# A hybrid RWKV-7 / mLSTM layer: scans in written order on every engine, and finishing work cut into parts

## The chip, the cores and the metric

The kernel runs on one core of a Trainium2 chip: TensorE (PE) for matmuls, VectorE (DVE), ScalarE (ACT), GpSimd (POOL), and SyncE (SP), which here only issues DMAs. The metric is the device time of one execution in microseconds; lower is better. Every number below is in us unless it says ns.

## The reference, cut to what matters

One layer of a bidirectional trunk over 128 context and 1024 latent tokens. A modulated RMSNorm feeds one input projection; its columns go to an RWKV-7 mixer, an mLSTM mixer and two sigmoid gates. Both mixers scan forward and backward; the latent scans start from states.

```
S = S*w_t - (S kk_t)(kk_t a_t)^T + v_t k_t^T;  y_t = S r_t          # RWKV-7, per head, both directions
y = group_norm(y_fwd + y_bwd) * lnx_g + lnx_b;  (y + bonus) * g
h = num / max(|den|, exp(-m));  C' = decay*C + sum_j w_j v_j k_j^T   # mLSTM, chunk of positions
h = group_norm(h_fwd + h_bwd) * gn_g * sigmoid(o)
merged = sigmoid(z_g)[r] * (y_r @ W_r) + sigmoid(z_g)[m] * (y_m @ W_m)
```

After that come an output projection, a residual and a gated convolution FFN.

## The kernel before, in words

Projections are computed with every weight split into a high and a low part (`whi` on ACT, `wlo` on DVE) and three products, 24 matmuls for one column group of 128. The regions of the program are: preparation and the first projections (to about 620 on the trace's time line), the RWKV scan (634 to 957), the mLSTM scan (971 to 1122), the rest of the gate products and the branches, then the FFN. The change touches the two scans alone.

**RWKV scan.** There are 18 steps n; each takes one chunk of 64 tokens per direction. `loads(n, d)` brings KA (two 128 KB DMAs), BKs and four TT pieces on SP, and XN on POOL's queue. KA comes from a ring of four buffers, two per step, so the loads for step n+1 need the buffers whose last reader is pY of step n-1. `scores(n+1, d)` makes psc and pbk of the coming step; ACT and DVE copy and mask them into A, KA, AB and BT. `merge` makes pmh and pmt (TT). `back(n)` is the recurrence: pP, pU (into suv), pN (into sn and the next suv), pY (into ysum). `between(n)` places the scores, the merge and the *gate products* (`fill(2)`: 2 times 12 matmuls pg of the 24 of a column group f, whose sigmoid goes to zraw and sgz) among the phases of `back`.

**Work carried by the scan.** `gates()` is a generator of six stages, called after steps 3, 4, 5, 6, 8 and 10, that prepares the mLSTM gates: small DMAs on SP (gi, gf, red, rr, mpd, mc, Mrd, dcd, decb), scans on DVE and Exp/Ln on ACT. `rpost(b)` finishes a block of 128 tokens of RWKV output (mean, variance, power on POOL, pgg and pgt on PE, yt): a first part after the step in POST, a second part in the next step's `between`.

**mLSTM scan.** There are 18 iterations i. `mfront` (two iterations ahead) adds the mask on POOL, takes Exp on ACT (MI), makes pmP and pmk, scales kw on ACT and multiplies MI by S on DVE. `mback` makes pmN and pmC, den, hs (h or hsum) and CN. `mfinish(c)` (from i = 10 on, and once at i = 1) makes mu on DVE, four squares on ACT (sqm), va, a power on POOL, h3, pmf and som.

**What sets the order.** PE's instructions keep the written order during both scans. On DVE, ACT, POOL and SP a scheduler chose the order at build time, except that the gate stages were kept in order (`pinned(gate)`). An instruction waits at the head of its engine's queue, and everything behind it on that engine waits too.

Of the kernel before, what the change touches and what calls it, by code (L numbers as in the profile page):

```python
# [16 lines left out]
NB = 9  # L17
# [40 lines left out]
def _body(tc, ctx, A, O, dbg, stop):  # L58
# [80 lines left out]
    Mrd = dram("Mrd", [2, 2, 36, 128])  # L139
# [225 lines left out]
    def split_w(srcs, nk, ncol, pool_=None, tag="w", bufs=2):  # L365
# [6 lines left out]
        nsplit[0] += 1  # L372
        if pool_ is None:
# [7 lines left out]
        return hi, lo  # L381

# [358 lines left out]
    def zg_groups(fs):  # L741

        w2s = {}

        def load(f):
            w2s[f] = split_w([kp(w_in[:, 3984 + 128 * f:4112 + 128 * f])], 8, 128)

        for i, f in enumerate(fs):
            if f not in w2s:
                load(f)  # L750
            sg = stage()
            for g in range(3):
# [19 lines left out]
    banks(pg=2, ps=3, pf=3)  # L772
# [10 lines left out]
    rp = pool("rpost", 1, mpc)  # L783
    cpc = ExitStack()
# [119 lines left out]
    def back(n, qs, suv, suv_next, parts):  # L904
# [57 lines left out]
    def rpost(b):  # L962
# [14 lines left out]
        gp.tensor_tensor(va, va, mhalf, op=ALU.pow)  # L977
        v.tensor_tensor(y, y, va.unsqueeze(2).to_broadcast([128, 8, 64]), op=ALU.mult)
        yield
        bon = rp.tile([128, 4, 128], F32, name="bon", tag="bon")  # L980
        pdma(bon, bond[:, :, bs].rearrange("p c t -> c p t"))
        for p in range(4):
            s.activation(bon[:, p, :], bon[:, p, :], AF.Identity, bias=P("rwkv_lnx_b", p))
# [14 lines left out]
        v.tensor_tensor(yt, pgg, yt, op=ALU.mult)  # L998
        pdma(yrd[:, :, bs].rearrange("p c t -> c p t"), yt)
# [5 lines left out]
    def gates():  # L1005
# [94 lines left out]

    def between(n):

        if n + 1 == len(ORDER):
            for i in range(3):
# [11 lines left out]
        if due:  # L1116
            due.pop(0)()
        fill(2)
# [13 lines left out]
    gate, due = gates(), []  # L1132
    pe.on = True
    for n in range(len(ORDER)):
# [3 lines left out]
        if n > 0 and n + 1 < len(ORDER):  # L1138
            fr[n + 1] = [loads(n + 1, d) for d in range(2)]
        sn = back(n, fr.pop(n), suv, None if n == 1 else nxt, between(n))  # L1140
        suv = nxt
        if n == 1:
            due.append(lambda sn=sn: finish_ctx(sn))
        if n in POST:
            r = rpost(POST[n])
            next(r)
            due.append(lambda r=r: next(r))
        if n in (3, 4, 5, 6, 8, 10):
            pinned(gate)
# [42 lines left out]
    def mload(d, c):  # L1192
        q = Chunk()
        q.d, q.c, q.vx = d, c, None
        q.qk = mp.tile([128, 8, 128], F32, name="qk", tag="qk", bufs=3)
        dma(q.qk, qkd[c])
        q.MI = mp.tile([128, 2, 4, 128], F32, name="MI", tag="MI", bufs=4)
        for x in range(2):
            src = Mrd[x, d].rearrange("(h c) t -> h c t", c=NB)[:, c, :]
            dma(q.MI[:, x], src.unsqueeze(0).to_broadcast([128, 4, 128]))  # L1200
        return q

    def values(q, dma_):
        q.vx = mp.tile([128, 4, 130], F32, name="vx", tag="vx", bufs=2)
        dma_(q.vx[:, :, 0:128], vmd[q.c])
        gp.memset(q.vx[:, :, 128:129], 1.0)

    def mfront(q):
# [3 lines left out]
        if q.vx is None:  # L1212
            values(q, dma)

        gp.tensor_tensor(dm, dm, mbig[:, d:d + 1, :].to_broadcast([128, 4, 128]), op=ALU.add)
        for h in range(4):
            s.activation(dm[:, h, :], dm[:, h, :], AF.Exp, scale=-1.0, bias=cols(gT[0], d, c)[:, h:h + 1])
# [50 lines left out]
    def mfinish(c):  # L1268
        h3 = hs_of(c)
# [3 lines left out]
        sq = mf.tile([128, 4, 128], F32, name="sqm", tag="sqm")  # L1273
        va = mf.tile([128, 4], F32, name="va", tag="va")
        for h in range(4):
            s.activation(sq[:, h, :], h3[:, h, :], AF.Square, bias=mu[:, h:h + 1], accum_out=va[:, h:h + 1])
        v.tensor_scalar(va, va, 1.0 / 128, 1e-5, op0=ALU.mult, op1=ALU.add)
        gp.tensor_tensor(va, va, mhalf[:, 0:4], op=ALU.pow)
        for h in range(4):
            v.tensor_scalar(h3[:, h, :], h3[:, h, :], mu[:, h:h + 1], va[:, h:h + 1], op0=ALU.add, op1=ALU.mult)  # L1280
        so = mf.tile([128, 4, 128], F32, name="som", tag="sqm")
        dma(so, sod[c])
# [4 lines left out]
        for h in range(4):  # L1287
            v.scalar_tensor_tensor(so[:, h, :], pt[:, h, :], P("mlstm_gn_g", h), so[:, h, :],
                                   op0=ALU.mult, op1=ALU.mult)
        dma(ymd[:, :, 128 * c:128 * c + 128].rearrange("h p t -> p h t"), so)  # L1290
# [39 lines left out]
    qs = [mload(*dc) for dc in SEQ[0:3]]  # L1330
    for q in qs[0:2]:
        values(q, pdma)
    sts = [state_loads(d) for d in range(2)]
    rps = [rpost(b) for b in (1, 8)]
    next(rps[0])
    for q in qs[0:2]:
        mfront(q)
    next(rps[1])
    fill(2)
    fins, half = [], []  # L1340
    for i, (d, c) in enumerate(SEQ):
# [287 lines left out]
```

## Time and profile before

| what | value |
|---|---|
| median of 3 runs (lowest to highest) | 2233.98 (2229.5 to 2241.99) |
| profiled execution, its own time | 2238.79 |
| its span (first to last instruction) | 2237.1 |
| PE busy, share of the span | 2086.1, 93% |
| DVE / ACT / POOL busy | 1374.4 / 818.7 / 569.2 |
| granted TensorE clock, mean | 0.972 |

The span is 1.7 below the execution's own time. Busy PE includes matmuls slowed by a lower clock, so PE's busy time is not its shortest time.

### The profile page before, as it was taken

How to read it: one execution, taken by the hardware profiler on the slowest of the kernel's cores; microseconds unless marked ns; L12 is line 12 of the kernel's file. 1: busy time of each engine (PE TensorE's matmuls, PEld its weight loads, DVE VectorE, ACT ScalarE, POOL GpSimd, SP SyncE). 2: the span in 40 equal slices, each digit the busy share in tenths (PEclk: the TensorE clock that was granted, in tenths of full speed). 3: DMA queues.
4: the chain of work that ended last, by engine and by line, in shares of the span. 5: the costliest groups of instructions: out<-in, count | busy, mean ns of one | idle time of the engine just before them, and what ended most of it. 6: DMA issues, size and time to landing. Idle time of an engine off the chain costs nothing. (4 is left out here: it accounts for less than half of the span.)

```text
span 2237.1 us, 39684 instructions
## 1 busy us (share of the span) xinstructions
PE 2086.1 (93%) x16307; PEld 1933.2 (86%) x16307; DVE 1374.4 (61%) x2131; ACT 818.7 (37%) x1595; POOL 569.2 (25%) x726
## 2 busy tenths in 40 slices
PE   5999998998888988979889999999999999999998
PEld 3998898888887877868878978999999999999996
DVE  3766688879745656563733365655565556565658
ACT  3664746364234433345431143522222222212223
POOL 2000098888722224255412212000000000000004
PEclk8999999999999999989999999999999999999999
DMA  9135354545555555367677552111111111111114
GB/s 267 50 83 134 100 138 108 144 122 143 151 146 133 137 133 137 110 201 217 194 250 199 162 188 76 57 57 48 47 48 57 48 48 48 57 39 44 41 57 169
DMA packets 387189, 256.67 MB, mean 115 GB/s; under 512 B 90529, under 2 KB 362053, under 8 KB 387008
## 3 DMA queue, kind: packets, MB, share of 16 engines
q1 hardware_dynamic: 239824, 140.96, 22.4%
q10 hardware_dynamic: 137056, 88.83, 13.5%
q0 software_dynamic: 10128, 24.35, 4.0%
q8 instruction: 128, 2.10, 0.4%
q14 instruction: 53, 0.43, 0.1%
HBM read 188.82 MB, written 65.25 MB: 114 GB/s over the span
## 5 line engine op out<-in xcount | busy, mean ns | idle before, releaser
L393 PE MATMUL pg<-act,whi 128*128 128x384 f32 (+1 forms) x3808 | 724.6, 337 | 0.5 <-DVE act L356 0.4
L393 PEld LDWEIGHTS pg<-act,whi 128*128 128x128 f32 (+1 forms) x3808 | 665.7, 188 | 12.7 <-DVE act L356 0.7
L393 PE MATMUL pg<-act,wlo 128*128 128x384 f32 (+1 forms) x1904 | 373.1, 336 | 7.6 <-DVE wlo L380 7.6
L393 PEld LDWEIGHTS pg<-act,wlo 128*128 128x128 f32 (+1 forms) x1904 | 332.9, 187 | 11.1 <-DVE wlo L380 8.0
L380 DVE TENSOR_TENSOR wlo<-wraw,whi 128x1024 fp32r<-128x1024 f32 x130 | 162.8, 1254 | 226.7 <-ACT whi L379 221.2
L47 DVE SCALAR_TENSOR_TENSOR ua<-uraw,par,ua 128x945 f32<-128x945 f32 (+2 forms) x176 | 214.6, 1219 | 39.0 <-ACT ua L1514 35.8
L1593 POOL TENSOR_TENSOR x<-facc,grow 128x512 f32<-128x512 f32 x16 | 23.5, 1490 | 809.1 <-DMA x<-x1d 799.0
L393 PE MATMUL pfd<-whi,f 128*128 128x512 f32 x792 | 226.1, 394 | 0.2 <-ACT f L1528 0.2
L379 ACT ACTIVATE whi<-wraw 128x1024 fp32r<-128x1024 f32 x130 | 136.7, 1053 | 158.2 <-PE pg L393 85.3
L393 PEld LDWEIGHTS pfd<-whi,f 128*128 128x128 f32 x792 | 147.0, 188 | 28.8 <-issue 1.6
L1591 DVE TENSOR_TENSOR facc<-pfd,facc 128x512 f32<-128x512 f32 x162 | 110.3, 686 | 50.6 <-PE pfd L393 50.6
L540 POOL TENSOR_TENSOR Lb<-Lb,tmp 96x31 f32<-96x31 f32 (+15 forms) x155 | 130.3, 841 | 12.2
L538 POOL TENSOR_TENSOR tmp<-La,Lb 96x31 f32<-96x31 f32 (+15 forms) x155 | 122.9, 793 | 27.4 <-DMA La<-Ad 15.6
L393 PE MATMUL pfd<-wlo,f 128*128 128x512 f32 x396 | 122.7, 391 | 0.0
L1518 ACT ACTIVATE ua<-ua 128x1152 f32<-128x1152 f32 x22 | 25.7, 1169 | 221.5 <-DVE ua L47 221.5
L69 PE MATMUL pg<-act,whi 128*128 128x384 f32 x496 | 103.3, 360 | 0.0
L1528 ACT ACTIVATE f<-ua 128x384 fp32r<-128x384 f32 x66 | 32.1, 518 | 192.9 <-DVE ua L1527 192.9
L69 PEld LDWEIGHTS pg<-act,whi 128*128 128x128 f32 x496 | 91.2, 202 | 1.1
L47 DVE SCALAR_TENSOR_TENSOR qacc<-zraw,par,qacc 128x945 f32<-128x945 f32 (+2 forms) x64 | 86.6, 1353 | 8.7 <-ACT qacc L596 8.2
L1462 PE MATMUL pwo<-whi,act 128*128 128x512 f32 x288 | 90.1, 392 | 1.1 <-ACT whi L379 1.1
L872 DVE TENSOR_TENSOR KA<-psc,msk 64x512 f32<-64x512 f32 x72 | 49.3, 684 | 66.4 <-ACT A L871 66.1
L393 PEld LDWEIGHTS pfd<-wlo,f 128*128 128x128 f32 x396 | 74.3, 188 | 16.5
(398 smaller groups left out, 3280.1 us busy)
## 6 DMA issues: line engine op xcount, KB each, us to landing
wraw<-in_w_in ACTq DMA_DIRECT2D x44, 512.0 KB
wraw<-in_ffn_up ACTq DMA_DIRECT2D x44, 512.0 KB
zraw<-in_ada_w SPq DMA_DIRECT2D x24, 512.0 KB
wraw<-in_ffn_down ACTq DMA_DIRECT2D x22, 512.0 KB
KRd<-KR SPq DMA_DIRECT2D x24, 384.0 KB
sgz<-zraw ACTq DMA_DIRECT2D x16, 576.0 KB
KA<-KRd SPq DMA_DIRECT2D x72, 128.0 KB
BKs<-BKd SPq DMA_DIRECT2D x36, 256.0 KB
```

Source lines behind the costliest of these rows:

```text
L47: v.scalar_tensor_tensor(o, img[:, r0 + i:r1 + i, c0 + j:c1 + j], wt, o, op0=ALU.mult, op1=ALU.add)
L69: return (lambda *a, **k: tc.keep_in_program_order(f(*a, **k))) if self.on else f
L379: s.activation(hi, raw, AF.Copy)
L380: v.tensor_tensor(lo, raw, hi.bitcast(F32), op=ALU.subtract)
L393: pe.matmul(out, wt(hw, k), at(ha, k), start=(i == 0), stop=(i == last))
L538: e.tensor_tensor(t3, L[:, j, i].unsqueeze(2).to_broadcast([NI, n, m]), X[:, j:j + 1, c].to_broadcast([NI, n, m]), op=ALU.mult)
L540: e.tensor_tensor(X[:, i, c], X[:, i, c], t3, op=ALU.subtract)
L872: v.tensor_tensor(q.KA[orr, :, h, :], sc_[h][orr], msk[orr, d:d + 1, :].to_broadcast([64, 4, 128]), op=ALU.mult)
L1462: pe.matmul(pts[b][q], AS[g][:, ha, k, 128 * o:128 * o + 128], wo2[k][hw][:, 0, 512 * q:512 * q + 512], start=(k == 0 and i == 0), stop=(k ...
L1518: s.activation(ua, ua, AF.Silu)
L1528: s.activation(f2[:, 0, gs], ua[:, gs], AF.Copy)
L1591: v.tensor_tensor(acc[:, b, qs], pt, acc[:, b, qs], op=ALU.add)
```

## The change: what it does

1. During both scans DVE, ACT, POOL and SP keep the written order too, not only PE and the gate stages. DMAs issued by POOL and ACT stay with the scheduler.
2. `fill(2)` before pmt becomes `fill(1)` behind the second scores and `fill(1)` behind pY; pmh moves ahead of pY. The PSUM banks of the scan are pg 1, ps 3, pf 4 (before: 2, 3, 3).
3. The next gate weight is loaded at the group's first product and split into `whi`/`wlo` at the third.
4. `rpost` is cut into five slots, all in the step after the one that produced the block.
5. Mrd is laid out so that a chunk's MI is one DMA of 128 rows by 4 KB (before: two, of 512-byte runs). Sixteen stores of 9x128 replace four of 36x128. The MI tiles take KA's ring; the first qk and two MI are loaded in the last RWKV step.
6. `mfinish` is cut into five parts over three iterations, and kw goes ahead of the Exp on ACT.

```diff
-    banks(pg=2, ps=3, pf=3)
+    banks(pg=1, ps=3, pf=4)
...
-            dma(Mrd[0, d], Ms[r])
-            dma(Mrd[1, d], it[r])
+            for x, t_ in enumerate((Ms, it)):
+                for h in range(4):
+                    dma(Mrd[d, :, x, h], t_[64 * d + NB * h:64 * d + NB * h + NB])
...
-        for d in range(2):
-            scores(n + 1, d, qs[d])
-            yield
+        scores(n + 1, 0, qs[0])
+        slot()
+        yield
+        scores(n + 1, 1, qs[1])
+        slot()
+        fill(1)
+        yield
         m = merge(qs)
         next(m)
-        if due:
-            due.pop(0)()
-        fill(2)
+        slot()
+        yield
+        if n == 2:
+            finish_ctx(ctx_sn[0])
+        slot()
+        fill(1)
         next(m)
         yield
...
-    pe.on = True
+    rest = (pe, v, s, gp, sy)
+    for e in rest:
+        e.on = True
...
         for h in range(4):
             s.activation(q.kw[:, h, :], pk[:, h, :], AF.Copy, scale=cols(gT[2], d, c)[:, h:h + 1])
+        for h in range(4):
+            s.activation(dm[:, h, :], dm[:, h, :], AF.Exp, scale=-1.0, bias=cols(gT[0], d, c)[:, h:h + 1])
...
-        for m in half:
-            next(m)
-        half = fins[0:1]
-        del fins[0:1]
-        for m in half:
+        for m in stores + old + new:
             next(m)
         if i + 2 < len(SEQ):
             mfront(qs[i + 2])
+        for m in new:
+            next(m)
         fill(1)
-        if done:
-            fins.append(mfinish(c))
+        for m in old:
+            next(m)
+        stores, old, new = old, new, [mfinish(c)] if done else []
```

**SP around the gate stage behind step 4.** First before, then after. `red<-bG` stores what a DVE chain makes; KA, BKs and TT are the loads of the scan.

```order
L75 DMA KA<-KRd 64x4x128 x4
L75 DMA BKs<-BKd 128x4x128
L75 DMA TT_5726<-Xtd 32x4x32 x4
L75 DMA TT_5728<-Xtd 32x4x32
L69 DMA red<-bG 36x2
L75 DMA BKs<-BKd 128x4x128
L75 DMA TT_5728<-Xtd 32x4x32 x2
L69 DMA red<-bG 36x2
```

```order
L69 DMA TT_5731<-Xtd 32x4x32 x4
L69 DMA red<-bG 36x2 x2
L69 DMA KA<-KRd 64x4x128 x2
L69 DMA BKs<-BKd 128x4x128
L69 DMA TT_5728<-Xtd 32x4x32 x4
L69 DMA KA<-KRd 64x4x128 x2
```

The four KA loads that stood ahead of both `red` stores now stand behind them, and the second direction's KA also behind BKs and four TT of the first.

**SP around the gate stages behind steps 6 and 8,** after the change: the stores s_m, mpd, the reload mc, and further on the stores of Mrd and dcd, each with what follows it. (Before, Mrd was four stores, and the KA loads of the coming step stood ahead of each of the two stages, but for one KA DMA ahead of mc.)

```order
L69 DMA s_m<-mm_7692 4x1
L69 DMA mpd<-mpv_7693 4x9
L69 DMA s_m<-mm_7701 4x1
L69 DMA mpd<-mpv_7702 4x9
L69 DMA mc<-mpd 36x1 x2
L69 DMA KA<-KRd 64x4x128 x2
```

```order
L69 DMA Mrd<-GG 9x128 x4
L69 DMA Mrd<-gf 9x128 x4
L69 DMA dcd<-dc 36x1
L69 DMA Mrd<-GG 9x128 x4
L69 DMA Mrd<-gf 9x128 x4
L69 DMA dcd<-dc 36x1
L69 DMA KA<-KRd 64x4x128 x2
```

Here too the scan's loads come behind the whole stage.

**DVE in the second half of the mLSTM scan,** one iteration before, then one after. mu, va and hsum<-hsum are the finishing of a chunk, MI<-S belongs to the chunk two iterations ahead.

```order
L1277 TENSOR_SCALAR va<-va 128x4
L1271 TENSOR_REDUCE mu<-hsum 128x4
L1280 TENSOR_SCALAR hsum<-hsum,mu,va 128x128 x4
L1250 TENSOR_TENSOR den<-pmN,gT_5716 128x4
L1272 TENSOR_SCALAR mu<-mu 128x4
L1230 TENSOR_TENSOR MI<-S,MI 128x512
L1251 SCALAR_TENSOR_TENSOR den<-pmN,den 128x4
L1265 TENSOR_TENSOR CN<-pmC,CN 128x4x129
L1252 RECIPROCAL den<-den 128x4
L1288 SCALAR_TENSOR_TENSOR som<-pmf,par,som 128x128
L1262 SCALAR_TENSOR_TENSOR hsum<-pmN,den,hsum 128x128 x4
```

```order
L69 TENSOR_TENSOR den<-pmN,gT_5716 128x4
L69 SCALAR_TENSOR_TENSOR den<-pmN,den 128x4
L69 RECIPROCAL den<-den 128x4
L69 SCALAR_TENSOR_TENSOR hsum<-pmN,den,hsum 128x128 x4
L69 TENSOR_TENSOR CN<-pmC,CN 128x4x129
L69 TENSOR_SCALAR hsum<-hsum,mu,va 128x128 x4
L69 TENSOR_REDUCE mu<-hsum 128x4
L69 TENSOR_SCALAR mu<-mu 128x4
L69 TENSOR_TENSOR MI<-S,MI 128x512
L69 TENSOR_SCALAR va<-va 128x4
L69 SCALAR_TENSOR_TENSOR som<-pmf,par,som 128x128 x4
```

mu and MI<-S, between which other work stood in the iteration before, are now neighbours, and den, hs and CN stand ahead of both.

**ACT in the same stretch:** one iteration before, then one after.

```order
L1276 ACTIVATE sqm,va<-hsum,mu 128x128 x4
L1229 ACTIVATE kw<-pmk,gT_5717 128x128 x4
L1217 ACTIVATE MI<-MI,gT_5715 128x128 x6
```

```order
L69 ACTIVATE sqm,va<-hsum,mu 128x128 x4
L69 ACTIVATE kw<-pmk,gT_5717 128x128 x4
L69 ACTIVATE MI<-MI,gT_5715 128x128 x4
```

The kinds keep their sequence, but before a run of six Exp reached ahead into a later chunk.

## Rows read from the trace of the kernel before

**Rows 1.** Windows by stretch: length, then each engine's busy time, granted clock, DMA share.
```profile
core 0: us, PE busy (x) PEld busy (x) DVE busy (x) ACT busy (x) POOL busy (x), PEclk, DMA share, GB/s
...
719.06:739.51 20.45, 17.68 (x293) 15.79 (x288) 11.19 (x25) 10.38 (x22) 5.43 (x13) 0.83 0.37 88
754.53:769.11 14.58, 14.29 (x295) 12.98 (x289) 7.71 (x13) 5.85 (x17) 3.84 (x7) 1.00 0.53 126
...
783.68:803.73 20.05, 16.38 (x294) 14.90 (x289) 8.21 (x14) 6.42 (x20) 6.20 (x11) 0.91 0.67 143
835.92:936.09 100.17, 85.48 (x1647) 77.55 (x1641) 67.68 (x132) 37.46 (x98) 34.46 (x46) 0.97 0.48 126
936.09:971.07 34.98, 28.29 (x318) 26.90 (x314) 17.47 (x27) 11.08 (x30) 15.91 (x21) 0.90 0.60 181
971.07:1002.80 31.73, 22.85 (x198) 21.30 (x197) 19.37 (x35) 14.90 (x46) 14.70 (x15) 0.84 0.62 191
1002.80:1059.09 56.29, 51.47 (x374) 50.57 (x373) 20.70 (x53) 33.02 (x110) 30.45 (x33) 0.94 0.70 212
1059.09:1111.60 52.51, 46.65 (x337) 44.89 (x336) 40.43 (x137) 26.94 (x106) 24.92 (x28) 0.97 0.63 192
1111.60:1152.77 41.17, 30.58 (x185) 28.46 (x185) 19.44 (x34) 16.12 (x26) 4.24 (x6) 0.91 0.86 284
```

**Rows 2.** Timeline of PE in a scan step without extra work.
```profile
769.11 1.15 PE L69 MATMUL pP<-suv,KA 128*64 128x64 f32 x32
770.19 1.16 PE L69 MATMUL psc<-KA,BKs 64*128 64x128 f32 x16
...
775.29 1.09 PE L69 MATMUL pN<-suv,BT 128*64 128x64 f32 x29 [0.29 <-ACT suv L919]
...
778.24 0.60 PE L69 MATMUL pmh<-XN,A 32*32 32x32 f32 x32
```

**Rows 3.** Timelines of SP, ACT and DVE around the gate stage behind step 4.
```profile
712.71 2.98 SPq L75 DMA_DIRECT2D KA<-KRd  x4
...
720.30 1.28 ACT L69 ACT_TABLE_LOAD   x1
...
722.54 1.28 ACT L69 ACT_TABLE_LOAD   x1
...
726.91 0.41 DVE L69 TENSOR_TENSOR_SCAN GG<-gi 64x128 f32<-64x128 f32 x1
```

**Rows 4.** Timeline of SP at the gate stages behind steps 6 and 8.
```profile
752.59 0.24 SPq L69 DMA_DIRECT2D mpd<-mpv  x1
...
755.35 1.26 SPq L69 DMA_DIRECT2D mc<-mpd  x2
...
786.09 0.32 SPq L69 DMA_DIRECT2D Mrd<-gf  x1
```

**Rows 5.** DMA issues in 634 to 957: KB each, median us from issue to landing.
```profile
suv<-Vd POOLq DMA_DIRECT2D x64, 128.0 KB, 3.8
```

**Rows 6.** Groups of DVE and ACT, 1059 to 1121: busy, mean ns, idle before, releaser.
```profile
L1271 DVE TENSOR_REDUCE mu<-hsum 128x4 f32<-128x512 f32 x8 | 5.4, 676 | 0.0
...
L1276 ACT ACTIVATE sqm<-hsum,mu 128x128 f32<-128x128 f32 x32 | 12.5, 390 | 21.2 <-DVE mu L1272 12.9 <-DMA ymd<-som 8.3
```

**Rows 7.** Timelines of DVE and ACT in one iteration of that half.
```profile
1096.75 1.12 DVE L1280 TENSOR_SCALAR hsum<-hsum,mu,va 128x128 f32<-128x128 f32 x4 [0.60 <-POOL va L1278]
...
1097.92 0.68 DVE L1230 TENSOR_TENSOR MI<-S,MI 128x512 f32<-128x512 f32 x1
...
1098.09 0.40 ACT L1276 ACTIVATE sqm<-hsum,mu 128x128 f32<-128x128 f32 x1 [3.25 <-DVE mu L1272]
...
1099.65 1.10 ACT L1229 ACTIVATE kw<-pmk,gT 128x128 f32<-128x128 f32 x4
```

**Rows 8.** Timeline of PE, 957 to 1000: two waits at the mLSTM scan's start.
```profile
964.86 1.09 PE L69 MATMUL pmk<-ident,qk 128*128 128x128 f32 x4 [5.62 <-DMA qk<-qkd]
...
980.96 1.09 PE L69 MATMUL pmi<-ident,cn 128*128 128x128 f32 x4 [5.08 <-issue]
```

More of the change, by code (lines that the diff above doesn't have):

```diff
@@ L138, in _body @@
     mpd = dram("mpd", [2, 4, NB])
-    Mrd = dram("Mrd", [2, 2, 36, 128])
+    Mrd = dram("Mrd", [2, NB, 2, 4, 128])
     dcd = dram("dcd", [2, 36])
@@ L932, in back @@
             v.tensor_tensor(sn[hr] if suv_next is None else suv_next[hr, :, h, 0], sn[hr], wl, op=ALU.mult)
+        next(parts)
         py = pss([128, 2, 4, LC], "pY")
@@ L977, in rpost @@
         gp.tensor_tensor(va, va, mhalf, op=ALU.pow)
+        bon = rp.tile([128, 4, 128], F32, name="bon", tag="bon")
+        pdma(bon, bond[:, :, bs].rearrange("p c t -> c p t"))
+        yield
         v.tensor_tensor(y, y, va.unsqueeze(2).to_broadcast([128, 8, 64]), op=ALU.mult)
         yield
[L980 to L983, printed above, removed]
         pgg = psf([128, 4, 128], "pgg")
@@ L993, in rpost @@
                               start=True, stop=True)
+        for p in range(4):
+            s.activation(bon[:, p, :], bon[:, p, :], AF.Identity, bias=P("rwkv_lnx_b", p))
         yt = rp.tile([128, 4, 128], F32, name="yt", tag="yt")
@@ L1099, in gates, with slot @@
         yield
+    def slot():
+        while late:
+            next(late.pop())
+        if due:
+            r = due[0]
+            next(r)
+            left[0] -= 1
+            if left[0] == 0:
+                late.append(due.pop(0))
+                left[0] = 4
     def between(n):
         if n + 1 == len(ORDER):
-            for i in range(3):
-                if due:
-                    due.pop(0)()
-                fill(2)
+            for i in range(4):
+                slot()
+                if i != 2:
+                    fill(2)
                 yield
@@ L1131, in _body @@
     init_state(None, suv)
-    gate, due = gates(), []
-    pe.on = True
+    gate, due, late, left, ctx_sn = gates(), [], [], [4], []
+    rest = (pe, v, s, gp, sy)
+    for e in rest:
+        e.on = True
+    first_m = []
     for n in range(len(ORDER)):
@@ L1139, in _body @@
             fr[n + 1] = [loads(n + 1, d) for d in range(2)]
+        if nxt is None:
+            qk0 = stage()[:, 0:1024].rearrange("p (a t) -> p a t", t=128)
+            dma(qk0, qkd[0])
+            for d in range(2):
+                MI = hp.tile([128, 2, 4, 128], F32, name="MI", tag="KA")
+                dma(MI, Mrd[d, 0].unsqueeze(0).to_broadcast([128, 2, 4, 128]))
+                first_m.append((qk0, MI))
         sn = back(n, fr.pop(n), suv, None if n == 1 else nxt, between(n))
@@ L1142, in _body @@
         if n == 1:
-            due.append(lambda sn=sn: finish_ctx(sn))
+            ctx_sn.append(sn)
         if n in POST:
-            r = rpost(POST[n])
-            next(r)
-            due.append(lambda r=r: next(r))
+            due.append(rpost(POST[n]))
         if n in (3, 4, 5, 6, 8, 10):
-            pinned(gate)
+            next(gate)
+    for r in late:
+        next(r)
+    for e in rest[1:]:
+        e.on = False
     cpc.close()
@@ L1190, in _body, with mload @@
         pass
-    def mload(d, c):
+    def mload(d, c, first=None):
         q = Chunk()
-        q.d, q.c, q.vx = d, c, None
+        q.d, q.c = d, c
+        q.vx = None
+        if first is not None:
+            q.qk, q.MI = first
+            return q
         q.qk = mp.tile([128, 8, 128], F32, name="qk", tag="qk", bufs=3)
         dma(q.qk, qkd[c])
[L1197 to L1200, printed above, removed]
-        return q
[L1203 to L1206, printed above, removed]
+        q.MI = hp.tile([128, 2, 4, 128], F32, name="MI", tag="KA")
+        dma(q.MI, Mrd[d, c].unsqueeze(0).to_broadcast([128, 2, 4, 128]))
+        return q
     def mfront(q):
@@ L1211, in mfront @@
         dm, qi = q.MI[:, 0], q.MI[:, 1]
-        if q.vx is None:
-            values(q, dma)
+        if (d, c) == (1, 0):
+            q.vx = qs[0].vx
+        else:
+            q.vx = mp.tile([128, 4, 130], F32, name="vx", tag="vx", bufs=2)
+            dma(q.vx[:, :, 0:128], vmd[c])
+            gp.memset(q.vx[:, :, 128:129], 1.0)
         gp.tensor_tensor(dm, dm, mbig[:, d:d + 1, :].to_broadcast([128, 4, 128]), op=ALU.add)
-        for h in range(4):
-            s.activation(dm[:, h, :], dm[:, h, :], AF.Exp, scale=-1.0, bias=cols(gT[0], d, c)[:, h:h + 1])
         if c not in Ss:
@@ L1329, in _body @@
     CNs = [state(d) for d in range(2)]
-    qs = [mload(*dc) for dc in SEQ[0:3]]
-    for q in qs[0:2]:
-        values(q, pdma)
+    qs = [mload(*dc, first=x) for dc, x in zip(SEQ[0:2], first_m)]
+    for e in rest[1:]:
+        e.on = True
     sts = [state_loads(d) for d in range(2)]
+    qs.append(mload(*SEQ[2]))
     rps = [rpost(b) for b in (1, 8)]
+    mfront(qs[0])
     next(rps[0])
-    for q in qs[0:2]:
-        mfront(q)
-    next(rps[1])
+    mfront(qs[1])
+    next(rps[0])
     fill(2)
-    fins, half = [], []
+    next(rps[0])
+    old, new, stores = [], [], []
     for i, (d, c) in enumerate(SEQ):
@@ L1348, in _body @@
             sts[d] = state(d, *sts[d])
-        for m in half:
-            next(m)
-        half = fins[0:1]
-        del fins[0:1]
-        for m in half:
+        if i == 0:
+            next(rps[0])
+            next(rps[1])
+        for m in stores + old + new:
             next(m)
@@ L1363, in _body @@
             CNs = sts
-    for m in half:
+    for m in stores + old + new:
         next(m)
-    for m in fins:
+    for m in new:
         next(m)
-        fill(2)
+    fill(1)
+    for m in old:
         next(m)
-    pe.on = False
+        next(m)
+    for m in new:
+        next(m)
+        fill(1)
+        next(m)
+        next(m)
+    for e in rest:
+        e.on = False
     if stop == "ym":
```

43 lines of the change are left out of this document (31 added, 12 removed).

## The prediction

> **What bounds the kernel now.** I read the windows by stretch first, since the change touches only about 634 to 1150 of a span of 2237.1. The reader should look there for stretches in which PE's busy time falls short of the length: whatever the other engines do, only those can shrink. A scan step without extra work is already full, 14.29 busy of 14.58; the two steps of 20.45 and 20.05 that carry gate stages, the five from 835.92 on that carry finishing work, the change from one scan to the other, and parts of the mLSTM scan are not [rows 1]. Then I read the timelines, for what PE waits for in a plain step and at the change of scans [rows 2, 8], for when SP issues loads and gate DMAs [rows 3, 4], and the groups and timelines of DVE and ACT in the second half of the mLSTM scan [rows 6, 7]. There PE has 46.65 busy in 52.51 while DVE has 40.43 [rows 1], so a worse sequence on DVE has little room before PE waits.
>
> 0.5% of this kernel, 11 us, is about what a measurement can tell from no change.
>
> **The change part by part.**
>
> *Gate stages on SP.* Written order puts each stage's DMAs ahead of the coming step's KA, and a DMA that waits holds all loads behind it. KA is read by psc, 1.08 after the step's pP (770.19 less 769.11) [rows 2]. Before, the four KA were on their way at 712.71, well ahead of the step at 719.06 [rows 3, 1].
>
> Stage behind step 4: ACT starts its first table load at 720.30, 1.2 into the step. Two loads of 1.28 and two short activations (0.40 each, taken like a square) make 3.4 [rows 3, 7]; DVE then runs per direction two prefix scans of 0.41 and three smaller pieces, estimated 1.3, 2.6 for both, and 0.3 ahead of them [rows 3]. That is 7.5 into the step, with overlap of the first store 7; two KA issues at 0.75 (2.98 for four) give 8.5, and the landing comes after that. No row has KA's landing: POOL's queue takes 3.8 for the same 128 KB [rows 5], the reload of mc was issued 2.76 after its store mpd (755.35 less 752.59) [rows 4]. With those ends psc waits till 11.3 to 12.3 against 1.1: about 10. The step becomes 14.3 + 10 plus some lost clock (0.17 of 20.45, 3.5, is lost there now [rows 1]): 26, +5.5.
>
> Stage behind step 6: its DVE work ends about as the step begins; two pairs of stores at 0.24 and a little more, 1.3, then 2.8 to mc and 1.3 for its two issues, 1.5 for KA and 2.8 to 3.8 landing [rows 3 to 5]: 9.7 at the long end, 7 if mc goes early; stall 6, +6 on a step of 14.58. Stage behind step 8: before, the first store of `gf` left at 786.09, 2.4 into the step; after, fourteen stores still follow from there at 0.4 (0.32 and a gap), 5.6, then KA as above, 12.5; stall 11, step 25.5 to 26, +5.5 to +6 on 20.05 [rows 1, 4]. Sum +18; the ends are 0 (all stages ready before the step) and +25.
>
> *Finishing in slots.* Five steps take 100.17 with 85.48 of PE work [rows 1]. The five slots spread the chain, but on one in-order DVE it still holds KA, AB, suv, sn and the finishing in a row, so I stay nearer the upper end: 95, -5, and -1 for the step that finishes block 0. Ends: -14.7 and 0.
>
> *Half gate products.* Twelve matmuls behind the second scores give ACT time for suv: the 0.29 ahead of pN [rows 2] goes on some nine plain steps, -2.6. But the time between pY's end and psc shrinks. Today pY ends at 778.24 and the next pP starts at 783.68; pmh, 24 gate matmuls and pmt fill these 5.4 [rows 1, 2]. With half the products and pmh moved ahead about 2.7 is left, and 1.08 from pP to psc: 3.8. KA can be issued only when pY is done and takes 1.5 + 2.8 to 3.8 (above), so it comes 0.5 to 1.5 late on nine steps, 5 to 14; the lower row, also on SP's queue, is the nearer, and 7 is taken. Ends: 0 (KA lands faster than both) and +14. It is covered by nothing: PE's next instruction is psc.
>
> *Change of scans.* qk and two MI are loaded in the last step, so the 5.62 wait for qk goes, and the 5.08 ahead of pmi is covered by finishing work and the earlier state loads [rows 8]. The last step could fall from 34.98 to 28.29, the first two iterations from 31.73 to 22.85 [rows 1]; chains of finishing on DVE remain, so 29 and 26: -12. Ends: -15.6 and 0.
>
> *mLSTM, first half.* 56.29 with 51.47 busy and a clock of 0.94 [rows 1]; fewer waits as kw and S come in order: -5. Ends: -8 (4.8 idle and 3.4 clock) and 0.
>
> *mLSTM, second half.* ACT's squares wait for mu, as they do today (12.9 of idle time) [rows 6]; but today DVE does MI<-S right at mu and den, CN, som and hs while ACT squares [rows 7]. After, DVE has mu, then MI<-S of a chunk whose Exp ACT does only after squares and kw. So the two engines alternate. DVE from den to mu: den about 0.3, hs and hsum 1.12 each, CN 0.68 like MI<-S, mu 0.68 and 0.1: 4.0. ACT: squares 1.56 (1098.09 to 1099.65), kw 1.10, Exp 1.2 (four of its size): 3.9. DVE: MI<-S 0.68, va 0.1, som 1.12 like hsum: 1.9 [rows 6, 7]. With some 0.1 for each of four handoffs, 10.2 per iteration, while PE's share is 46.65 over eight, 5.8 [rows 1]. Iterations 12 to 15 take 10.2 each, 11 (no hsum and som yet) 7.9, 16 and 17 (no kw, Exp, MI) 7.2, 10 6.0: 69.1 against 52.51, +16.5. Ends: 0 and +20.
>
> *Rest.* Split and load of gate weights, fewer and larger MI loads (DMA share 0.63 to 0.70 there [rows 1], nobody waits on MI), the shared vx, more Mrd stores apart from the wait above: nothing, hidden by PE's gate products; if that cover is gone, it is in the ranges above. The stretch to 1152.77 has 10.6 without PE work [rows 1]; loads in another order there may take 2 off (0 to 5).
>
> Sum: +18 - 6 - 2.6 + 7 - 12 - 5 + 16.5 - 2 = +13.9, taken as +13. On the profiled execution's 2238.8 that is 2252; it ran 5 above the median of the runs, 2234, so I forecast **2247**.
>
> **A price from the clock.** In the second half a wait of over 4 will precede most iterations' matmuls. Today the whole stretch loses 0.03 of 52.51, 1.6 [rows 1]; if each of five such waits cost that, 8 would be added, but PE then has spare time in the same iteration, so I count nothing. The Trainium skill (TensorE: Matmul & The Clock Gate, Part 1) says that the clock's default is the halved one and that activity releases it, so gaps are paid twice; by it the forecast would be the clock rival's below.
>
> **The rivals.**
> *SP keeps up (faster).* Place: the KA loads of the coming step. If gate stages end before their step starts and KA lands within 3.7 of pY, +18 and +7 go: 2247 - 25 = 2222. For it: gate DVE work comes ahead of the step's own on in-order engines, and PE reads KA late enough today. Against: ACT's table loads alone end 4.7 into the step (722.54 and 1.28 against 719.06) [rows 3]. It decides where KA's issue precedes the step's pP.
> *Ends pay for all (no change).* The change of scans and the finishing reach nearer their limits, -15 and -10: 2247 - 7 = 2240, or a little under.
> *Clock (slower).* Each second-half wait costs 1.6 on the alternating path as well: 2255.
> *KA late in every step (slower).* +14 in place of +7, and one more us at BKs and TT, which now come behind KA: 2255.
>
> **How the numbers follow.** Forecast 0.32 (own range 2240 to 2258), SP keeps up 0.24, ends pay 0.22, clock 0.12, KA late 0.10. The range takes in 2222 with 12 below for its ends (finishing, start) and 2255 with 17 above (gate stages at +25, second half at +20): 2210 to 2272. Faster by over 0.5% is below 2223: half of SP keeps up lies just under, and parts of the ends' cases beyond it, 0.26. Within 0.5% (to 2245): ends pay and the forecast's lower third, 0.32. Slower: the rest, 0.42.
>
> **What would show it.** Right: psc waiting for KA in the three steps after gate stages for 6 to 11; steps from 835.92 shorter by about 1 each; no wait for qk; iterations 12 to 15 of about 10 with ACT sqm behind DVE mu and DVE MI<-S behind ACT. Wrong: KA issued ahead of pP in those steps, second-half iterations of about 6, or waits ahead of psc in each plain step.

## The result

The changed kernel takes 2315.86 us (median of 4 runs, 2312.28 to 2317.67) against 2233.98: the ratio is 1.0342, with a 95% interval of 1.0316 to 1.0369. It is slower, as forecast, but by 82 where 13 were forecast, and outside the range (2210 to 2272). The profiled execution took 2315.49, its span is 2313.5 (before: 2237.1).

The windows of the changed kernel that answer to [rows 1]: length, busy time of each engine, granted clock, DMA share. The first is the scan from the first pP to the last, then the steps behind the gate stages 4 and 8, the five steps with finishing, the last step, mLSTM iterations 0 and 1, 2 to 9, 10 to the start of 17, and what follows up to the branch products.

```profile
624.80:988.53 363.73, 283.54 (x5210) 256.91 (x5204) 183.68 (x345) 116.84 (x300) 94.81 (x150) 0.89 0.48 112
721.57:751.07 29.50, 16.64 (x293) 15.03 (x288) 11.84 (x25) 11.35 (x23) 2.58 (x6) 0.77 0.34 82
811.01:846.16 35.15, 17.10 (x294) 15.48 (x289) 8.38 (x18) 6.66 (x20) 6.55 (x12) 0.71 0.30 83
881.80:988.53 106.73, 89.53 (x1647) 81.56 (x1641) 70.37 (x136) 36.55 (x97) 36.16 (x47) 0.94 0.58 138
988.53:1015.99 27.46, 26.55 (x317) 25.36 (x313) 10.99 (x21) 9.46 (x26) 10.01 (x13) 1.00 0.61 195
1015.99:1060.98 44.99, 26.70 (x197) 24.91 (x197) 22.70 (x41) 14.41 (x43) 14.70 (x15) 0.73 0.24 75
1060.98:1115.22 54.24, 50.49 (x374) 49.53 (x373) 22.73 (x53) 33.38 (x112) 28.52 (x32) 0.94 0.70 234
1115.22:1181.47 66.25, 49.75 (x297) 46.19 (x297) 40.33 (x116) 26.36 (x96) 27.89 (x31) 0.84 0.48 158
1181.47:1226.69 45.22, 38.22 (x225) 35.50 (x225) 26.36 (x56) 20.87 (x42) 6.99 (x8) 0.89 0.72 241
```

Compared stretch by stretch, from the first pP to the branch products (in the kernel before the scan runs from 634.19 to 936.09, iteration 10 starts at 1059.09 and 17 at 1106.13):

| stretch | before | after | change | forecast |
|---|---|---|---|---|
| start of the scan | 634.19 | 624.80 | -9.4 | 0 |
| scan, first pP to last | 301.90 | 363.73 | +61.8 | +16.4 |
| last RWKV step | 34.98 | 27.46 | -7.5 | -6 |
| iterations 0, 1 | 31.73 | 44.99 | +13.3 | -6 |
| iterations 2 to 9 | 56.29 | 54.24 | -2.1 | -5 |
| iterations 10 to the start of 17 | 47.04 | 66.25 | +19.2 | +14.9 |
| from there to the branch products | 46.64 | 45.22 | -1.4 | -0.4 |
| sum | | | +73.9 | +13.9 |

Nearly the whole difference (76.4 between the spans) lies here, and 62 of it in the scan. What PE waits for there, from the waits of 624.8 to 988.5 (total, times, longest):

```profile
PE psc L69 <- DMA BKs<-BKd: 63.1, 14, 18.1
```

One wait, fourteen times, makes up as much as the scan has lost; in the kernel before, PE's waits ahead of psc were 13.3 in all, 11.8 of them for ACT and DVE. Two SP timelines show how it comes about. First a step without extra work, then the one behind gate stage 8. Columns: start, duration, queue, DMA; for PE the wait in brackets.

```profile
789.47 1.27 SPq L69 DMA_DIRECT2D KA<-KRd  x2
790.79 0.60 SPq L69 DMA_DIRECT2D BKs<-BKd  x1
791.44 1.93 SPq L69 DMA_DIRECT2D TT<-Xtd  x4
793.47 1.25 SPq L69 DMA_DIRECT2D KA<-KRd  x2
794.76 0.60 SPq L69 DMA_DIRECT2D BKs<-BKd  x1
...
795.20 1.25 PE L69 MATMUL psc<-KA,BKs 64*128 64x128 f32 x16 [0.88 <-PE pP L69]
...
800.59 1.25 PE L69 MATMUL psc<-KA,BKs 64*128 64x128 f32 x16 [2.47 <-DMA BKs<-BKd]
...
811.29 2.61 SPq L69 DMA_DIRECT2D Mrd<-GG  x4
814.30 1.72 SPq L69 DMA_DIRECT2D Mrd<-gf  x4
...
821.82 0.29 SPq L69 DMA_DIRECT2D dcd<-dc  x1
822.20 1.25 SPq L69 DMA_DIRECT2D KA<-KRd  x2
823.50 0.61 SPq L69 DMA_DIRECT2D BKs<-BKd  x1
...
830.22 2.17 PE L69 MATMUL psc<-KA,BKs 64*128 64x128 f32 x16 [18.05 <-DMA BKs<-BKd]
```

In the plain step SP stands idle until pY lets KA's buffers go (SP waits for pY 14 times in the scan, 120.8 in all), and then issues everything for the next step in one row: the BKs of the second direction leaves at 794.76 and psc can start only at 800.59. Behind the gate stage, the same row starts 11 after the first Mrd store.

In the late mLSTM iterations, DVE and ACT (the ACT rows first):

```profile
1149.12 0.40 ACT L69 ACTIVATE sqm<-hsum,mu 128x128 f32<-128x128 f32 x1 [7.03 <-DVE mu L69]
...
1151.10 1.12 ACT L69 ACTIVATE kw<-pmk,gT 128x128 f32<-128x128 f32 x4
1152.10 1.28 ACT L69 ACTIVATE MI<-MI,gT 128x128 f32<-128x128 f32 x4
...
1148.85 0.17 DVE L69 TENSOR_SCALAR mu<-mu 128x4 f32<-128x4 f32 x1
1153.46 0.69 DVE L69 TENSOR_TENSOR MI<-S,MI 128x512 f32<-128x512 f32 x1 [4.44 <-ACT MI L69]
...
1157.42 2.12 DVE L69 TENSOR_SCALAR hsum<-hsum,mu,va 128x128 f32<-128x128 f32 x4
```

ACT is idle until mu, DVE is idle until the Exp behind squares and kw, in turn: the alternation that was forecast.

At the start of the mLSTM scan, PE's two long waits and what POOL does ahead of the second:

```profile
1024.76 1.97 PE L69 MATMUL pgt<-ident,ysum 64*64 64x64 f32 x32 [5.03 <-DVE den L69]
...
1047.61 1.98 PE L69 MATMUL pgt<-ident,ysum 64*64 64x64 f32 x32 [7.86 <-DVE den L69]
...
1037.38 0.69 DVE L69 TENSOR_TENSOR MI<-S,MI 128x512 f32<-128x512 f32 x1 [3.49 <-ACT MI L69]
1037.99 0.68 DVE L69 TENSOR_REDUCE yva<-sqy 128x8 f32<-128x512 f32 x1
...
1043.44 4.02 DVE L69 TENSOR_TENSOR ysum<-ysum,yva 128x512 f32<-128x512 f32 x1 [4.57 <-POOL yva L69]
...
1040.91 0.80 POOL L995 DMA_DIRECT2D bon<-bond  x1 [7.79 <-issue]
1041.73 1.68 POOL L69 TENSOR_TENSOR yva<-yva,mhalf 128x8 f32<-128x8 f32 x1
```

The profile names den, but what pgt reads is ysum, whose multiplication ends at 1047.46, just before pgt. pgt stands in PE's queue ahead of the next iteration's products and waits for a chain of ACT, DVE and POOL: yva's sum is written behind MI<-S and so waits for Exp; the power waits behind the issue of bon's load on POOL; and the multiplication of ysum takes 4.02.

### The profile page after: what moved, and what is told of

The parts are those of the page before. It is cut to its first block, busy times and chain, and to the rows that moved or that the text cites. A ratio compares the mean times of both kernels' runs of the same rounds, so it can differ in the third digit from the quotient of the medians.

```text
span 2313.5 us, 39614 instructions
## 1 busy us (share of the span) xinstructions
PE 2109.0 (91%) x16307; PEld 1950.9 (84%) x16307; DVE 1381.5 (60%) x2131; ACT 821.5 (36%) x1595; POOL 567.8 (25%) x723
## 5 line engine op out<-in xcount | busy, mean ns | idle before, releaser
L384 DVE TENSOR_TENSOR wlo<-wraw,whi 128x1024 fp32r<-128x1024 f32 (+1 forms) x119 | 149.6, 1258 | 192.0 <-ACT whi L383 191.4
L383 ACT ACTIVATE whi<-wraw 128x1024 fp32r<-128x1024 f32 (+1 forms) x119 | 125.1, 1053 | 146.1 <-PE pg L400 83.7
L547 POOL TENSOR_TENSOR Lb<-Lb,tmp 96x31 f32<-96x31 f32 (+15 forms) x155 | 132.8, 857 | 12.2
L545 POOL TENSOR_TENSOR tmp<-La,Lb 96x31 f32<-96x31 f32 (+15 forms) x155 | 120.1, 775 | 27.3 <-DMA La<-Ad 15.5
L69 PE MATMUL psc<-KA,BKs 64*128 64x128 f32 x544 | 49.8, 323 | 66.3 <-DMA BKs<-BKd 63.1
L69 PEld LDWEIGHTS psc<-KA,BKs 64*128 64x128 f32 x544 | 42.8, 224 | 69.8 <-issue 62.6
L867 POOL DMA_DIRECT2D XN<-Xnd x72 | 39.4, 554 | 223.8 <-PE pmh L69 211.0
```

The lines of the kernel that those rows point to most:

```text
L69: return (lambda *a, **k: tc.keep_in_program_order(f(*a, **k))) if self.on else f
L545: e.tensor_tensor(t3, L[:, j, i].unsqueeze(2).to_broadcast([NI, n, m]), X[:, j:j + 1, c].to_broadcast([NI, n, m]), op=ALU.mult)
L547: e.tensor_tensor(X[:, i, c], X[:, i, c], t3, op=ALU.subtract)
```

## The experiments

All edits are to the changed kernel unless it says otherwise. Times without a ratio are single executions. The kernel before took 2236.51 (one execution) beside the first four of these kernels, on the same chip; 2236.56 (median of 19) beside the one with SP alone free and the three from "All three together" on; 2237.84 (median of 7) beside the other two.

**BKs and TT a step ahead.** `loads` is cut in two; only KA and XN stay behind pY.

```diff
         scores(n + 1, 1, qs[1])
         slot()
+        if n + 2 < len(ORDER):
+            fr[n + 2] = [loads_b(n + 2, d) for d in range(2)]
         fill(1)
...
-            fr[n + 1] = [loads(n + 1, d) for d in range(2)]
+            fr[n + 1] = [loads(n + 1, d, fr[n + 1][d]) for d in range(2)]
...
```

> The changed kernel, but BKs and TT of the step after next are issued on SP behind the second scores, so that only the four KA loads and XN are left for the time behind pY. Theory A (the ten SP loads of a step stand in one burst behind pY, and psc waits for the BKs at its end): the plain steps of 17.1 to 18.7 and 20.9 fall to 14.6 to 15.5, psc waits for nothing or for KA for less than 1, and the scan (363.7 from the first pP to the last, in the changed kernel) loses 25 to 35. Theory B (the ring of four KA buffers alone is what comes late): psc still waits 2 or more in each plain step, now for KA, and the scan loses less than 10. Both: the steps behind the gate stages 4 and 8 (29.5 and 35.2) keep 8 or more of their waits, since KA still stands behind the stages.

2283.49. The scan and the two gate steps:

```profile
626.76:953.38 326.62, 276.27 (x5208) 250.89 (x5203) 181.83 (x342) 117.22 (x300) 93.82 (x149) 0.92 0.49 125
707.29:736.11 28.82, 17.21 (x294) 15.59 (x289) 11.84 (x25) 11.36 (x23) 2.59 (x6) 0.76 0.34 85
785.06:818.39 33.33, 16.91 (x293) 15.29 (x289) 8.38 (x18) 6.65 (x20) 6.57 (x12) 0.74 0.31 88
```

The scan falls by 37, a little more than was expected; most plain steps are 14.2 to 14.4, shorter than the 14.58 of [rows 1]. So KA alone comes in time from its ring of four, and the burst was what came late; theory A holds, and theory B falls. The gate steps stay long, as expected.

**Gate stages behind the loads.** The call of `next(gate)` moves from the end of step n to behind the loads at the head of step n+1.

```diff
+        if n - 1 in (3, 4, 5, 6, 8, 10):
+            next(gate)
...
-        if n in (3, 4, 5, 6, 8, 10):
-            next(gate)
```

> The changed kernel, but each gate stage is written behind the loads of the coming step instead of ahead of them; only SP's sequence changes. Theory A (the stage's waiting DMAs hold the loads): the steps of 29.5 and 35.2 fall to 18 to 20 like their neighbours, the one of 21.2 by 2 or 3, together 25 to 30. Rival (those steps are long because ACT's table loads and DVE's gate work stand ahead of the step's own in written order): they fall by less than 8 together, and psc, pU or pN wait for ACT or DVE there.

2295.77. The scan is 336.1, less by 27.6; the step of 29.50 is now 18.06 and that of 35.15 is 22.56 (18 to 20 was expected), but the one after it, which was 19.48, became 22.45, since now its loads wait. The stage's place on SP is the cause; moving it also moves part of the wait to the next step.

**mLSTM: front ahead of the squares.** `mfront` of the chunk two ahead is called before the part with mu and squares, and va with its power at the start of the next iteration.

```diff
+        for m in old:
+            next(m)
         CNs[d] = mback(qs[i], CNs[d])
...
-        for m in stores + old + new:
+        for m in stores + old:
             next(m)
         if i + 2 < len(SEQ):
             mfront(qs[i + 2])
...
```

> The changed kernel, but in an mLSTM iteration the front of the chunk two ahead (kw, Exp, MI times S) is written ahead of mu and the squares, and va with its power goes to the start of the next iteration. Theory A (DVE and ACT take turns: mu, squares, kw, Exp, MI times S, in written order): the iterations of 11.3 fall to 6 to 7.5, the second half (66 from iteration 10 to the end of the scan) to 45 to 52. Rival (these iterations are long because DVE's work with the cut finishing is itself longer than PE's, or because the clock falls): they stay above 9.

2322.47, no gain. Iterations 10 to the start of 17 fall from 66.25 to 58.41 only; single ones take 7.8 to 12.2. The expectation failed. POOL's timeline shows that one turn was replaced by another:

```profile
1163.26 1.02 POOL L69 TENSOR_TENSOR va<-va,mhalf 128x4 f32<-128x4 f32 x1 [4.51 <-DVE den L69]
1164.25 1.06 POOL L69 TENSOR_TENSOR CN<-CN,decb 128x516 f32<-128x516 f32 x1
...
1165.30 1.26 POOL L69 TENSOR_TENSOR MI<-MI,mbig 128x512 f32<-128x512 f32 x1
```

The power waits for va, which waits for the squares; CN, the mask addition of the next chunk, its Exp on ACT and MI<-S on DVE wait behind it, and mu behind these. The start-to-start distance of `den` is 9.0 (1154.06 to 1163.03), close to the sum of that ring. DVE is nearly as late by itself: Exp ends at 1167.88, and hsum, 2.43 long beside POOL's operations, ends at 1168.38, just as MI<-S starts. The 7.8 gained there were lost again: the scan started 3.4 later and was 1.8 longer, 5.9 were lost between iteration 17 and the branch products, where a wait of 7.3 for the sigmoid of a gate product stands, and some 6 behind them, where the edit changes nothing. These losses weren't pursued.

**Written order on PE alone.** All of the restructuring, but DVE, ACT, POOL and SP as the scheduler has them, with the gate stages in order as before.

```diff
-    rest = (pe, v, s, gp, sy)
+    rest = (pe,)
...
-            next(gate)
+            pinned(gate)
```

> The changed kernel with its code order, half products, slots, layout and early mLSTM loads, but written order kept on PE alone (and inside the gate stages, as before the change); DVE, ACT, POOL and SP are again the scheduler's. Theory A (the written order on the other engines is what costs): the time falls back by most of the 80, to 2225 to 2250. Rival (the restructuring itself, such as half products, the five slots and the split Mrd stores, costs): it stays above 2280.

2234.27, against 2236.51 of the kernel before. The written order on the other engines is the loss; half products, five slots, split stores and early loads together are worth about nothing without it, as gains and losses offset each other: the scan is 306.41 (301.90 before), the last step 37.66 (34.98), iterations 0 and 1 are 28.34 (31.73), 2 to 9 48.82 (56.29).

**SP alone free.**

```diff
-    rest = (pe, v, s, gp, sy)
+    rest = (pe, v, s, gp)
```

> The changed kernel with written order on PE, DVE, ACT and POOL, and SP alone left to the scheduler. Theory (the scan's loss is SP's sequence, the mLSTM scan's loss that of DVE, ACT and POOL): the scan comes down from 363.7 to 305 to 320, while the first two mLSTM iterations stay at about 45 and the late ones above 11; total 2255 to 2275. Rival (the compute engines' order costs in the scan too): the scan stays above 335.

2253.7, just below what was expected.

```profile
625.54:926.80 301.26, 272.11 (x5209) 246.75 (x5203) 182.81 (x343) 116.75 (x300) 94.16 (x150) 0.95 0.55 135
...
954.26:998.07 43.81, 26.53 (x198) 24.73 (x198) 22.61 (x41) 14.41 (x43) 14.72 (x15) 0.69 0.34 105
```

The scan falls by 62.5, to what it was before the change, while iterations 0 and 1 stay at 43.81 and the late ones at 11.2 to 11.7. The scan's loss is SP's, the mLSTM scan's is not.

**SP in order, nothing else (an edit to the kernel before).**

```diff
-        for e in (v, s, gp, sy):
+        for e in (v, s, gp):
             e.on = False
...
     pe.on = True
+    sy.on = True
...
     for n in range(len(ORDER)):
...
             pinned(gate)
+    sy.on = False
     cpc.close()
```

> The kernel before, with nothing changed but that SP keeps the written order during the RWKV scan (KA, BKs, TT of a step behind the gate stage that is written ahead of them). Theory: SP's sequence alone does what the scan of the changed kernel shows: steps behind the gate stages 4 and 8 of 26 to 36, plain steps of 16 to 19, the scan 345 to 370 instead of 302, total 2280 to 2305. Rival (it takes the written order of DVE and ACT, or the half products that leave less time behind pY, as well): the scan stays below 325, with psc waiting in the gate steps alone.

2287.12, 49 more than the 2237.84 of the kernel before on that chip. The waits of its scan (634.4 to 986):

```profile
PE psc L69 <- DMA BKs<-BKd: 49.4, 10, 15.7
```

Its windows of the scan and of the two gate steps:

```profile
634.41:985.95 351.54, 280.88 (x5207) 255.55 (x5203) 181.88 (x345) 116.98 (x301) 93.36 (x151) 0.89 0.45 110
736.33:765.25 28.92, 15.63 (x294) 14.17 (x288) 11.33 (x25) 10.50 (x22) 4.45 (x12) 0.76 0.32 81
816.24:848.73 32.49, 16.74 (x295) 15.24 (x289) 8.21 (x14) 6.54 (x20) 5.98 (x11) 0.74 0.43 109
```

SP's sequence alone costs 50 in the kernel before, with the same wait. Most of it lies in the steps behind gate stages; in step 3 psc waits 7.9, as the store of the context state (s_rwkv, issued at 688.53 after a wait for DVE) stands ahead of KA (689.89). The plain steps hardly grow: 1, 8 and 11 take 14.6 to 14.8, where 16 to 19 was expected. The 12 between 351.5 and 363.7 fit the half products, which leave less time between pY and psc (steps 1, 6, 8, 10 and 11 take 14.6 to 17.4 here, 16.2 to 20.9 in the changed kernel), but no run took the half products out alone, nor parted them from the written order of DVE and ACT.

**All three together.** The SP cures of the first two runs, and a second rearrangement of the mLSTM iteration (`mfront` cut in two, the power behind the mask addition).

```diff
+            mfront(qs[i + 2], True)
+        for m in old:
+            next(m)
+            next(m)
+        for m in new:
+            next(m)
+        if i + 2 < len(SEQ):
+            mfront2(qs[i + 2])
...
```

> The changed kernel, written order everywhere, with BKs and TT a step ahead, gate stages behind the loads, and a second rearrangement of the mLSTM iteration: va at its start, the power behind POOL's mask addition, kw and Exp ahead of the squares, MI times S behind mu. (The first one left a turn through POOL: va, power, CN, mask addition, Exp.) Theory (the two SP terms are independent and add up; without a turn the late iterations are as long as PE's or DVE's work): scan 300 to 308, iterations from 12 on 6 to 7, first two mLSTM iterations still about 45; total 2225 to 2240. Rival (one wait only replaces the other): scan above 315 or iterations above 9, total above 2250.

2245.55, ratio 1.0041 (1.0021 to 1.0061), above the expected 2225 to 2240. The scan adds up: 307.84, and the first two mLSTM iterations are 43.9, as expected. Iterations 10 to the start of 17 are 55.92, and those from 12 on 7.3 to 10.1, so the mLSTM part of the expectation failed again. In iteration 14 DVE waits 0.99 for va's power ahead of hsum; the power stands on POOL behind vx's clearing, which starts at 1088.79, as pmC ends (pmC reads vx). hsum itself then takes 2.81 (1.12 in [rows 7]) beside two operations of POOL. What of the rest is POOL's was not settled.

**The SP cures, and the mLSTM scan free.** As above for the scan; in the mLSTM scan written order is kept on PE alone, by leaving out the lines that turn it on for the rest.

```diff
     qs = [mload(*dc, first=x) for dc, x in zip(SEQ[0:2], first_m)]
-    for e in rest[1:]:
-        e.on = True
     sts = [state_loads(d) for d in range(2)]
```

> The two SP cures in the scan in written order, and in the mLSTM scan written order on PE alone. Theory (the start of the mLSTM scan is long because the finishing of two RWKV blocks and the first fronts share DVE, ACT and POOL in written order): from the last RWKV step to iteration 2 65 to 68 instead of 72, late iterations as in the run with PE alone in order, 53 for eight; total 2215 to 2230. Rival (the scheduler's order does no better at the start once the last step is in written order): 70 or more there, total above 2235.

2218.12, ratio 0.9918 (0.9889 to 0.9946) to the kernel before: it beats both kernels, the one before by 0.8%. Scan, last step, iterations 0 and 1, 2 to 9, 10 to the start of 17, and step 10 of the scan:

```profile
627.08:929.18 302.10, 271.78 (x5209) 246.19 (x5204) 183.15 (x344) 116.79 (x300) 96.73 (x152) 0.95 0.55 135
929.18:960.38 31.20, 28.15 (x317) 26.95 (x313) 21.34 (x30) 15.32 (x43) 19.15 (x21) 0.95 0.69 208
960.38:988.61 28.23, 22.91 (x197) 21.48 (x197) 15.55 (x42) 13.71 (x43) 11.13 (x11) 0.88 0.49 152
988.61:1037.30 48.69, 47.97 (x374) 47.35 (x373) 19.47 (x48) 29.32 (x97) 27.32 (x30) 1.00 0.82 259
1037.30:1084.52 47.22, 42.51 (x296) 40.06 (x297) 37.04 (x116) 25.27 (x97) 25.13 (x28) 0.96 0.59 189
785.78:812.69 26.91, 17.71 (x297) 15.74 (x292) 9.15 (x18) 6.74 (x20) 4.75 (x9) 0.81 0.48 115
```

From the last step to iteration 2 it needs 59.4, where the changed kernel needs 72.4 and the one before 66.7, and less than the 65 to 68 that were expected. The scan is back at its old length, but one wait is left in it: step 10 takes 26.91 (17.62 before), and 8.0 of that is psc's wait for KA, which SP issues at 790.87, 5.1 into the step, behind gate stage 8 and the BKs and TT that go with this KA. Shorter steps elsewhere make up for it (step 9 takes 15.5, 20.05 before). With SP free (the last run below) step 10 is as long, 27.17, so it isn't the written order on SP alone that holds KA there; no run went after it.

**The start free, the rest in the rearranged order.**

```diff
             CNs = sts
+            for e in rest[1:]:
+                e.on = True
...
```

> Both: the SP cures, the scheduler's order in the first two mLSTM iterations, and from then on the rearranged iteration in written order. Theory: 302 for the scan, 65 to 68 to iteration 2, 49 for iterations 2 to 9, 50 to 53 for the last eight; total 2210 to 2225, below the kernel before by 0.5 to 1%. Rival (the start in free order holds back what follows): above 2230.

2231.86, ratio 0.9973 (0.9953 to 0.9993): above the expected 2210 to 2225, and by its time the rival's. But iterations 2 to 9 are 49.7, so nothing is held back there; the start is 57.0, the scan 302.76. Between the two profiled executions (2231.22 and 2211.84) lie 19.4: the late iterations, 54.74 to the start of 17, lose 7.5 to the run before, the way from there to the branch products 4.6 (45.77 against 41.14), and 9.7 lie behind, where the two kernels are alike; that part has no cause here.

**SP free throughout, the mLSTM scan free but for PE.** Written order on DVE, ACT and POOL in the RWKV scan only, without either SP cure.

> The changed kernel with written order on DVE, ACT and POOL in the scan only; SP free throughout, and in the mLSTM scan written order on PE alone. Theory (SP's sequence and the mLSTM scan's compute order are the whole loss, and the two cures for SP do no more than the scheduler does): scan 300 to 305, from the last RWKV step to iteration 2 58 to 61, eight late iterations 52 to 54, total 2212 to 2222, like the run with the two SP cures (2218). Rival (the loads written a step ahead are worth more than the scheduler's): 2228 or more.

2217.54, ratio 0.9921 (0.99 to 0.9941): the same as with the two cures. The scan is 304.90, last step and iterations 0 and 1 59.2, so the scheduler's SP does as well as the loads written a step ahead.

## Why the prediction was wrong

The direction was right, and so were two places (the gate stages, the second half of the mLSTM scan), but the sum (+13.9) is a fifth of what the same stretches show (+73.9). Four terms make up the 60 between them: the first two mLSTM iterations (19), the plain scan steps (16), the gate stages (13) and the finishing (12). By its own steps:

*Gate stages on SP, +18.* The mechanism was right and shown from both sides. Forecast waits 10, 6 and 11; with only KA behind the stage (the first run) 11.6, 3.6 and 16.4; in the changed kernel 12.9, 5.4 and 18.1, as BKs follows KA. The three steps cost +30.8. Where the size was off most is the last (+15.1): I started the fourteen stores that follow at 2.4 into the step with 0.4 each and so had KA's issue 8 in; SP issued KA at 822.20, 11.2 in, as the stage's eighteen DMAs took 10.8 from 811.29 on, 0.6 each. (Two slips in the sum: for the stage behind step 6 the terms add up to 10.7 at the long end, not 9.7, and the three stages to 17 to 17.5, taken as 18.) The Trainium skill (DMA: Bandwidth & Descriptors, Anatomy of one DMA — SWDGE (gpsimd) path) says that DMA engines don't wait on semaphores, the wait is on the issuing sequencer ahead of dispatch. By that rule loads behind a waiting store go no earlier, and the trace agrees: the last pY of the step before ends at 808.3, yet KA at 822.20 follows dcd at 821.82.

*Half gate products and KA, +7.* This step failed in its mechanism. It priced KA alone behind pY, 0.5 to 1.5 late on nine steps. With KA alone there (the first run) psc waits for nothing in steps 1, 4, 6, 8 and 11. But in written order BKs and four TT of each direction, which the scheduler issued a step ahead, stand behind KA too, so that psc waits for the second BKs, not for KA: steps 1, 3, 4, 6 and 8 are 2.5 to 5.9 longer than before, against 0.8 forecast, steps 10 and 11 1.6 to 1.9, 23 for the seven. (In step 3 the store s_rwkv, at 678.26, stands ahead of the loads as well.) The order shown with the change has it (KA, BKs, four TT, KA), and the rival "KA late in every step" named BKs and TT at one us in all. It should have been the sum of all issues ahead of the last load that psc reads: two KA, BKs, four TT, two KA, BKs, 5.9 (789.47 to 795.36), and 5.2 from there to psc.

*Finishing, -6.* Wrong in sign: 106.73 against 100.17 for the five, and still 104.4 with the cure for BKs and 103.5 with SP free. In these two runs pgt waits 2.2 to 3.3 for ysum in each of these steps; with written order on PE alone it does not, and the five take 98.6. So the overlap was wrong: the written order of DVE, ACT and POOL costs here instead of helping; which of the three was not tried apart. I stayed near the upper end by feel.

*Change of scans, -12.* The last step was right (27.46, forecast 29). For the first two iterations I took 26, near PE's own work, and gave no walk of the chain; they are 44.99, the largest miss of all. The path was wrong: pgt waits 5.0 and 7.9 for the finishing of RWKV blocks. The cause lies in the written order there, as the free start shows (25.9 to 28.2); which of the three delays in the rows above weighs most was not tried apart.

*mLSTM, second half, +16.5.* Right in kind and in place, and nearly in size: iterations 12 to 15 take 11.2 to 11.7 (forecast 10.2), the stretch to iteration 17 +19.2 (forecast 14.9). The rest is hsum at 2.12 where 1.12 was taken and the squares at 1.98 (1149.12 to 1151.10) where 1.56 was. In part the sum is luck: iteration 11 takes 5.2 for 7.9, and 16 takes 10.4 for 7.2. The clock (0.84 in this stretch) did not decide, as DVE and ACT set the pace. The two runs that rearranged the iteration shortened the stretch (58.4 and 55.9 for 66.25) but did not bring it to PE's length, so the turn of DVE and ACT is read from the rows; what the runs show is that the written order costs here (47 to 48 with the scheduler's).

*First half and rest.* Iterations 2 to 9: -2.1 for -5. The -9.4 ahead of the scan wasn't forecast: the waits of PE before it differ from run to run (the first pP is at 625 to 628 in all runs with written order on ACT, at 632 to 634 in those with the scheduler's, where a wait of 2.9 to 4.4 for BT stands ahead of the first scores); a third to a half of it is shown by that wait.

*SP keeps up,* the rival for faster, fell: KA is never issued ahead of pP in the gate steps. But its price shows what the order cost: with SP free, the scan is 62 shorter.

## What to carry to other kernels

When a queue is put in written order, list everything that stands between the event that frees it and the last transfer that the waiting instruction reads, add the issue times, and do this for the plain step first, since it is multiplied by the number of steps. Loads whose buffers are free early belong ahead of the wait for the one that isn't. And where two in-order engines hand work to each other twice in an iteration, moving one operation makes another turn (here through POOL) unless the whole ring is drawn: the scheduler's order did better on the mLSTM scan than two orders by hand.

## What the runs showed of the hardware that was not expected

A DVE operation can be stretched by POOL. hsum<-hsum, four of 128x128, takes 1.12 in [rows 7] and 2.12 at 1157.42 in the changed kernel, where POOL's MI<-qk,MI runs from 1157.68 for 1.26. The same ysum multiplication of 128x512 takes 0.69 at 1003.49, 1.55 at 1023.06 and 4.02 from 1043.44. For the second, POOL's operation and DVE's own; for the third, POOL's three operations in that time:

```profile
1023.01 1.04 POOL L69 TENSOR_TENSOR CN<-CN,decb 128x516 f32<-128x516 f32 x1
1023.06 1.55 DVE L69 TENSOR_TENSOR ysum<-ysum,yva 128x512 f32<-128x512 f32 x1 [1.66 <-POOL yva L69]
...
1043.38 1.04 POOL L69 TENSOR_TENSOR CN<-CN,decb 128x516 f32<-128x516 f32 x1
...
1044.44 1.25 POOL L69 TENSOR_TENSOR MI<-MI,mbig 128x512 f32<-128x512 f32 x1
1045.66 1.25 POOL L69 TENSOR_TENSOR MI<-qk,MI 128x512 f32<-128x512 f32 x1
```

POOL's last operation ends at 1024.05 and at 1046.91, DVE's at 1024.61 and at 1047.46, 0.56 and 0.55 later, a little less than its undisturbed length. The Trainium skill (SBUF — State Buffer, SBUF: two separate sides) says that a DVE operation with two inputs in SBUF and a POOL operation that reads SBUF take a shared pair of ports as a lock, and the other one blocks; for the ysum multiplication the trace agrees, and it fits DVE waiting for three POOL operations in a row. hsum's operation has one such input and two columns of scalars; for it the rows show the overlap alone.

The issue of one BKs on SP mostly takes 0.60 behind KA in the burst, and 0.38 to 0.39 in the kernel with BKs and TT a step ahead and in the kernel before; no run shows why.
